# Another order of the quads, other banks and more raw tiles in the gate blocks of a mixer kernel; one gate job moved

## The chip, the cores and the metric

The kernel runs on one core of a Trainium2 chip. The metric is device time in microseconds (us). The kernel before took 2747.88 us, the median of three runs from 2747.08 to 2752.04.

## The reference, cut to what matters

One layer of a sequence mixer on x of 256 rows and 4096 columns, all in float32:

```
h = rms_norm(x)                                    # 256 x 4096
proj = h @ w_in                                    # 4096 x 22560, split by columns into
u, v, z_gm (2048 each), q k v of the delta rule (2048 each), z_dn, b, a, gate_gm, gate_dn (4096 each)
y_gm = (gelu(u) * spatial(layer_norm(gelu(v))) * silu(z_gm)) @ w_br_gmlp      # 2048 x 4096
y_dn = (rms_norm(gated_delta_rule(conv(q), conv(k), conv(v))) * silu(z_dn)) @ w_br_dn
x = x + (sigmoid(gate_gm) * y_gm + sigmoid(gate_dn) * y_dn) @ w_out           # 4096 x 4096
out = rms_norm(x)
```

## The kernel before, in words

All weights stream from HBM once. A product in float32 precision is made of three TensorE matmuls of a high and a low part: xh*wh, xh*wl and xl*wh. A raw weight tile holds 128 x 1024 numbers (0.5 MB); ScalarE casts it to the high part `wh` and VectorE subtracts to make the low part `wl` (`split`, L182 to L188; in the gate blocks `cut`, L254). The 256 rows of x are the stationary operand, in two halves m of 128, so a matmul covers 128 x 128 by 512 columns and adds into one PSUM bank. There are eight banks: six in the pool `pm` (name `acc`) and two in `ps` (name `side`, handed out by `bank()`). The small matmuls of the other stages use `side`.

`stream` (L279) works through a list of jobs, cut into pieces. An ordinary `Job` is 512 columns of a weight: a piece is one raw tile, 12 matmuls, and a job of 4096 rows has 16 pieces in two banks. A `Block` is a pair of gate jobs, 1024 columns, worked through in 16 quads of 256 rows (two raw tiles). A quad named in `SEVEN` is computed with seven products in place of eight: `quad_split` (L258) forms sums and differences of the raw quarters on VectorE (L263, L264, L268, L269) and four pieces a, b, d, c bring 3 + 6 + 6 + 6 matmuls with prepared sums of x (`gforms`). Any other quad has two pieces, n0 and n1, of 12 matmuls. A block thus has 8 x 21 + 8 x 24 = 360 matmuls in eight accumulators, P1 to P8 (`block_acc`, L203); n pieces use P8, P4, P2, P3. Before, the quads of seven are 0, 2, ..., 14, so a block begins with a quad of seven and ends with one of eight. `sums_out` (L984) adds the eight accumulators into four outputs as each of them gets its last matmul: P1, P6, P7, P5 (twice), P4, P2, P3, P8 (L990 to L998).

`make` (L318) splits pieces ahead of the matmuls: up to four pieces (not counting a) and five pieces of the list, in four tiles each of `wh` and `wl`. `get` (L294) issues the raw loads on SyncE's queue (SP), in order, up to a number of tiles ahead, into five tiles `raw` of pool `wp` and, for blocks alone, one more of pool `px`. A raw tile is given back when the last piece that reads it is split.

All other work is written as generators in two queues, `lanes`; after each 12 matmuls `step` (L122) advances the head of each queue by one yield. Lane 0 holds what follows each job (`done_...`), lane 1 the delta rule (`ba_gen`, `dn_gen`). The written order is not the issued order: a planner that simulates the program arranges the instructions of each engine, by its own estimate of when each is ready, and gives out the slots of a pool as they come free.

The order of jobs: two gate jobs (0, 2), six blocks (12 gates), four groups of v, k, q and z_dn of the delta rule, four jobs v, then u and z_gm four times in turn, gates 13 and 15, sixteen jobs `w_br_...` and eight jobs `w_out`. A v job's `done_v` is followed, after the last one, by `ln_gen` (L517), which normalizes `vg` when `open_b` (L478), at the end of the last `dn_gen`, has opened the pool `pb`; `done_u` calls `need_b` (L495), which steps the lanes until then. `done_z` multiplies 128 x 128 matrices with `vg` (L576). `done_gate` (L971) takes the sigmoid and stores the gate. Gate 13 opens the last pool, `pc` (`open_c`, L1024), and queues the loads of the eight tiles `yr` (L1034), their casts (L1037) and differences (L1039), which the jobs `w_br_...` use as `ys`.

Of the kernel before, what the change touches and what calls it, by code (L numbers as in the profile page):

```python
# [17 lines left out]
P = 128  # L18
# [11 lines left out]
SUB = 32  # L30
TAIL = 5
WARM = 9
SEVEN = tuple(range(0, 16, 2))


class Job:
# [25 lines left out]
def trunk(ctx, tc, t):  # L62
# [25 lines left out]
    upr = cst.tile([P, P], F32, name="upr")  # L88
    low = cst.tile([P, P], F32, name="low")
    lowr = cst.tile([P, P], F32R, name="lowr")  # L90
    ones = cst.tile([P, P], F32, name="ones")
    half = cst.tile([P, 8], F32, name="half")
    rstd = cst.tile([P, 2], F32, name="rstd")
    dng = cst.tile([P, P], F32, name="dng")
# [11 lines left out]
    pres = {(q, g): dr.tile([S + 3, NC], F32, name=f"pre{q}{g}") for q in "kqv" for g in range(4)}  # L106
    sgs = [dr.tile([P, 2, NC], F32, name=f"sgs{c}") for c in range(16)]

    V.memset(ones, 1.0)
    V.memset(half, -0.5)  # L110

    def after(tiles, src):
# [87 lines left out]

    def block_acc():  # L203
        acc = {n: pm.tile([P, 512], F32, name="acc") for n in ("P1", "P6", "P7", "P5", "P4", "P2")}
        acc["P3"], acc["P8"] = bank(), bank()
        return acc

    def plain(job, k, m):
        a, r = job.src(k)
# [69 lines left out]
    def stream():  # L279
# [8 lines left out]
        for p in pieces:  # L288
            order += [r for r in p.raws if r not in order[-2:]]
        raws, home, sp, acc, late = {}, {}, {}, None, []  # L290
        room = {"wp": 5, "x": 1}
        state = dict(got=0, made=0, pairs=0, mm=0)

        def get(upto):  # L294
            while state["got"] < min(upto, len(order)):
                n = state["got"]
                j, k = order[n]
                quad = isinstance(j, Block)
                where = "wp" if room["wp"] else "x" if room["x"] and quad else None
                if where is None:  # L300
                    return
                if n > 3:
                    first_x(n)
                room[where] -= 1
                home[j, k] = where
                if not quad:
                    raws[j, k] = fetch(j, k, n == 0)
                else:
                    raw = (wp if where == "wp" else px).tile([P, KPD, NC], F32, name="raw",
                                                             bufs=5 if where == "wp" else 1)  # L310
                    nc.sync.dma_start(out=raw, in_=j.w[k * P:(k + 1) * P, j.col:j.col + 2 * NC].rearrange(
                        "p (c n) -> p c n", c=2))
                    raws[j, k] = raw
                if n < 4:
                    first_x(n)
                state["got"] += 1

        def make():  # L318
            p = pieces[state["made"]]
            n = order.index(p.raws[-1])  # L320
            get(n + (4 if p.kind == "std" else 5))
            if state["made"] == 0:
                sp[0] = split0(raws[p.raws[0]])
            elif p.kind == "std":
                split_x(state["made"])
                sp[state["made"]] = split(raws[p.raws[0]], state["made"] >= len(pieces) - TAIL)
            else:
                sp[state["made"]] = quad_split(p, [raws.get(r) for r in p.raws])
            for r in p.retire:
                raws.pop(r)  # L330
                room[home.pop(r)] += 1
            state["made"] += 1
            state["pairs"] += p.kind != "a"
# [637 lines left out]
    def done_gate(i):  # L971
        def f(acc):
            z = (pc.tile([P, 2, NC], F32, name="sg", bufs=4) if pc else
                 pb.tile([P, 2, NC], F32, name="gu", bufs=2) if pb else px.tile([P, 2, NC], F32, name="sg", bufs=3))

            def gen():
                for m in range(2):
# [46 lines left out]
    def open_c():  # L1024
        nonlocal pc
        done_by()
        phv.close()
        phb.close()
        pc = phc.enter_context(tc.tile_pool(name="pc", bufs=1, reuse_waits="tile"))

        def gen():
            for i in range(8):
                yr = pc.tile([P, 4, S], F32, name="yr", bufs=1)
                nc.sync.dma_start(out=yr, in_=(ygs + yds)[i])  # L1034
                ys[i] = pc.tile([P, 2, 4, S], F32R, name=f"ys{i}")
                yield 2
                A.copy(ys[i][:, 0], yr)  # L1037
                yield
                V.tensor_tensor(out=ys[i][:, 1], in0=yr, in1=ys[i][:, 0].bitcast(F32), op=ALU.subtract)  # L1039
                yield  # L1040
        lanes[1].append(gen())

    sig, part = {}, {}

    def before_br(i):
        def f():
            sig[i] = pc.tile([P, 2, NC], F32, name="sg", bufs=4)
            nc.sync.dma_start(out=sig[i], in_=sgs[i])
        return f

    def done_br(i):
        d, second = i // 2, i % 2

        def f(acc):
            s = sig.pop(i)

            def gen():
                for m in range(2):
                    V.tensor_tensor(out=s[:, m], in0=acc[m], in1=s[:, m], op=ALU.mult)
                if not second:  # L1060
                    part[d] = s
                    yield
                    return
# [1 line left out]
                for m in range(2):  # L1065
                    V.tensor_tensor(out=s[:, m], in0=s[:, m], in1=q[:, m], op=ALU.add)
                yield
                tt = pc.tile([P, 2, 4, P], F32, name="yr", bufs=1)
                for m in range(2):
                    sm, ms = heads(s[:, m]), slice(m * P, (m + 1) * P)  # L1070
                    yield from turn(sm, sm, tt[:, m])
# [101 lines left out]
    for c in range(4):  # L1173
        jobs.append(Job(win, U0 + c * NC, KT, xsrc, done_u(c)))
        jobs.append(Job(win, ZG0 + c * NC, KT, xsrc, done_z(c)))
    for i in (13, 15):
        jobs.append(Job(win, GD0 + i // 2 * NC, KT, xsrc, done_gate(i), open_c if i == 13 else None))
    for i in range(16):
        d, second = i // 2, i % 2
        jobs.append(Job(t["w_br_dn"] if second else t["w_br_gmlp"], d * NC, KT // 2,  # L1180
                        (lambda k, s=second * 4: (ys[s + k // 4], k % 4)), done_br(i), before_br(i)))
    for c in range(8):
# [55 lines left out]
```

## Time and profile before

| | |
|---|---|
| runs | 2747.08, 2747.88, 2752.04 us |
| the profiled execution | 2753.06 us, its span 2751.3 us |
| busy share of the span | TensorE 98%, weight loads 80%, VectorE 67%, ScalarE 53%, GpSimd 1% |
| mean granted TensorE clock | 0.996 |
| HBM | 569.16 MB read, 24.19 MB written, 216 GB/s |

Every time below is from the profiled execution, counted from the start of its span. A row of a timeline gives start, duration, engine, line, operation, output and inputs, and in brackets how long the engine was idle before it and what released it. A matmul's start is recorded; its end is modelled, and matmuls overlap, so the distance of starts tells how fast they run.

### The profile page before, as it was taken

The page shows a single profiled execution, that of the slowest core. Times are in us where ns is not written, and L with a number is a line of the kernel's source. Part 1 is how long each engine was busy: PE and PEld are TensorE (multiplying, and loading weights), DVE is VectorE, ACT ScalarE, POOL GpSimd, SP SyncE. Part 2 cuts the span into 40 slices and gives each one's busy share as a digit, 9 for nine tenths or more (in the row PEclk, how much of TensorE's full clock was granted, in tenths as well). Part 3 has the DMA queues.
Part 4 walks back from the last instruction along what each step waited for, and adds up shares of the span by engine and source line. Part 5 has one row for each costly group of instructions (what it writes and reads, how often), then busy time and mean ns, then how long its engine had stood idle before and what let it go on. Part 6 is the DMA issues. An engine that isn't in the chain of part 4 may idle for free.

```text
span 2751.3 us, 33611 instructions
## 1 busy us (share of the span) xinstructions
PE 2697.4 (98%) x12241; PEld 2208.1 (80%) x12241; DVE 1843.7 (67%) x2476; ACT 1453.0 (53%) x2023; POOL 40.1 (1%) x40
## 2 busy tenths in 40 slices
PE   9999999999999999999999999999999999999998
PEld 7777777788878778778878887888888888888886
DVE  8788888886676867865885656645556666655544
ACT  7555555554564555554655545545544655644443
POOL 0000000000000000000010000000000000000000
PEclk9999999999999999999999999999999999999999
DMA  9666666568777777875875666676776666576665
GB/s 352 198 192 202 202 206 216 177 218 263 220 225 236 239 221 219 260 215 168 294 201 171 199 182 198 193 207 198 218 273 211 224 214 219 177 243 216 207 215 168
DMA packets 300719, 595.58 MB, mean 216 GB/s; under 512 B 33636, under 2 KB 47972, under 8 KB 300168
## 3 DMA queue, kind: packets, MB, share of 16 engines
q1 hardware_dynamic: 300264, 593.28, 68.7%
q8 instruction: 96, 1.57, 0.2%
q14 instruction: 71, 0.58, 0.1%
q10 hardware_dynamic: 288, 0.15, 0.0%
HBM read 569.16 MB, written 24.19 MB: 216 GB/s over the span
## 4 chain that ended last, share of the span: by engine, by line
PE 67%; DVE 12%; DMA 12%; issue 4%; ACT 3%; SPq 1%; POOL 0%; DVEq 0%; POOLq 0%; ACTq 0%
PE acc L198 20%; PE acc L197 20%; PE acc L199 20%; DMA raw<-w_in 6%; DVE wl L256 3%; DVE wl L187 2%; PE acc L235 1%; PE acc L236 1%; PE acc L234 1%; DMA tok<-preq 1%; ACT wh L186 1%; DMA preq<-tok 1%; DVE tok L712 1%; DVE tt L264 1%; PE side L235 1%
## 5 line engine op out<-in xcount | busy, mean ns | idle before, releaser
L187 DVE TENSOR_TENSOR wl<-raw,wh 128x1024 fp32r<-128x1024 f32 x762 | 925.8, 1221 | 655.3 <-ACT wh L186 652.0
L186 ACT CAST wh<-raw 128x1024 fp32r<-128x1024 f32 x762 | 794.9, 1052 | 893.5 <-PE acc L199 822.0
L198 PE MATMUL acc<-wl,xs 128*128 128x512 f32 x2540 | 993.7, 391 | 9.3 <-DVE wl L187 9.1
L199 PE MATMUL acc<-wh,xs 128*128 128x512 f32 x2540 | 990.4, 390 | 0.0
L197 PE MATMUL acc<-wh,xs 128*128 128x512 f32 x2540 | 984.5, 392 | 5.7 <-ACT wh L186 5.3
L198 PEld LDWEIGHTS acc<-wl,xs 128*128 128x128 f32 x2540 | 478.0, 188 | 115.4 <-DVE wl L187 17.8
L197 PEld LDWEIGHTS acc<-wh,xs 128*128 128x128 f32 x2540 | 477.2, 188 | 108.1 <-ACT wh L186 8.7
L199 PEld LDWEIGHTS acc<-wh,xs 128*128 128x128 f32 x2540 | 477.7, 188 | 98.9
L198 PE MATMUL acc<-wl,ys 128*128 128x512 f32 x512 | 199.2, 389 | 0.0
L199 PE MATMUL acc<-wh,ys 128*128 128x512 f32 x512 | 199.2, 389 | 0.0
L255 ACT CAST wh<-raw 128x1024 fp32r<-128x1024 f32 x144 | 149.4, 1050 | 92.3 <-PE side L236 77.3
L197 PE MATMUL acc<-wh,ys 128*128 128x512 f32 x512 | 195.8, 389 | 0.0
L256 DVE TENSOR_TENSOR wl<-raw,wh 128x1024 fp32r<-128x1024 f32 x144 | 172.3, 1220 | 10.1 <-ACT wh L255 9.8
L235 PE MATMUL acc<-wl,xs 128*128 128x512 f32 x288 | 114.2, 396 | 4.1 <-DVE wl L256 4.0
L256 DVE TENSOR_TENSOR wl<-tt,wh 128x1024 fp32r<-128x1024 f32 x96 | 116.3, 1219 | 1.9 <-ACT wh L255 1.8
L236 PE MATMUL acc<-wh,xs 128*128 128x512 f32 x288 | 112.8, 392 | 0.0
L197 PEld LDWEIGHTS acc<-wh,ys 128*128 128x128 f32 x512 | 96.1, 188 | 20.1
L198 PEld LDWEIGHTS acc<-wl,ys 128*128 128x128 f32 x512 | 96.1, 188 | 19.9
L199 PEld LDWEIGHTS acc<-wh,ys 128*128 128x128 f32 x512 | 96.1, 188 | 19.9
L255 ACT CAST wh<-tt 128x1024 fp32r<-128x1024 f32 x96 | 99.3, 1047 | 21.6 <-PE acc L236 12.1
L234 PE MATMUL acc<-wh,xs 128*128 128x512 f32 x288 | 97.4, 392 | 0.0
L255 ACT CAST s<-raw 128x512 fp32r<-128x512 f32 x48 | 29.8, 621 | 125.0 <-DMA raw<-w_in 125.0
(270 smaller groups left out, 2308.2 us busy)
## 6 DMA issues: line engine op xcount, KB each, us to landing
raw<-w_in SPq DMA_DIRECT2D x703, 512.0 KB
raw<-w_out SPq DMA_DIRECT2D x128, 512.0 KB
raw<-w_br_gmlp SPq DMA_DIRECT2D x64, 512.0 KB
raw<-w_br_dn SPq DMA_DIRECT2D x64, 512.0 KB
cw<-conv_w SPq DMA_DIRECT2D x48, 256.0 KB
sgs<-sg SPq DMA_DIRECT2D x16, 512.0 KB
sg<-sgs SPq DMA_DIRECT2D x16, 512.0 KB
tok<-prev SPq DMA_DIRECT2D x12, 512.0 KB
```

The source lines that it names most:

```text
L186: A.copy(h, raw)
L187: V.tensor_tensor(out=l, in0=raw, in1=h.bitcast(F32), op=ALU.subtract)
L197: T.matmul(acc[m], lhsT=xh, rhs=h[:, kk], start=f, stop=False)
L198: T.matmul(acc[m], lhsT=xh, rhs=l[:, kk], start=False, stop=False)
L199: T.matmul(acc[m], lhsT=xl, rhs=h[:, kk], start=False, stop=e)
L234: T.matmul(acc[name], lhsT=xh, rhs=h[:, i], start=f, stop=False)
L235: T.matmul(acc[name], lhsT=xh, rhs=l[:, i], start=False, stop=False)
L236: T.matmul(acc[name], lhsT=xl, rhs=h[:, i], start=False, stop=e)
L255: A.copy(h, src)
L256: V.tensor_tensor(out=l, in0=src, in1=h.bitcast(F32), op=ALU.subtract)
L264: V.tensor_tensor(out=t12[:, 1], in0=t12[:, 0], in1=r1[:, 0], op=ALU.subtract)
L712: V.tensor_tensor(out=h[:, m], in0=h[:, m], in1=cw, op=ALU.mult)
```

## The change

Six edits. `SEVEN` becomes 1, 3, 4, 6, 8, 9, 11, 13: still eight quads, but a block begins with quad 0 and ends with quads 14 and 15 of eight products, and 3, 4 and 8, 9 are neighbours. `block_acc` takes P3 and P8 from `side` in odd blocks and P6 and P7 in even ones, and asks for the banks in another order. Pool `px` has three raw tiles in place of one, and `get` looks two tiles further ahead in blocks. Gate 13 runs between the last v and the first u, with its output tile in pool `pv`, and gate 15 opens `pc`. The `yr` tiles become two, their generator has two yields per tile in place of four and begins with the tiles of the delta rule; the `w_br_dn` job of each pair runs first, and the second `w_br` job waits until all of that generator has been written. The unused tile `ones` and its memset go.

```diff
-SEVEN = tuple(range(0, 16, 2))
+XRAW = 3
+SEVEN = (1, 3, 4, 6, 8, 9, 11, 13)
-    ones = cst.tile([P, P], F32, name="ones")
-    V.memset(ones, 1.0)
+    nblk = [0]
     def block_acc():
-        acc = {n: pm.tile([P, 512], F32, name="acc") for n in ("P1", "P6", "P7", "P5", "P4", "P2")}
-        acc["P3"], acc["P8"] = bank(), bank()
-        return acc
+        nblk[0] += 1
+        apart = ("P6", "P7") if nblk[0] % 2 == 0 else ("P3", "P8")
+        return {n: bank() if n in apart else pm.tile([P, 512], F32, name="acc")
+                for n in ("P8", "P4", "P2", "P3", "P1", "P6", "P5", "P7")}
-        room = {"wp": 5, "x": 1}
+        room = {"wp": 5, "x": XRAW}
-                                                             bufs=5 if where == "wp" else 1)
+                                                             bufs=5 if where == "wp" else XRAW)
-            get(n + (4 if p.kind == "std" else 5))
+            get(n + (4 if p.kind == "std" else 4 + XRAW))
@@ done_gate
-                 pb.tile([P, 2, NC], F32, name="gu", bufs=2) if pb else px.tile([P, 2, NC], F32, name="sg", bufs=3))
+                 pv.tile([P, 2, NC], F32, name="sg") if pv else px.tile([P, 2, NC], F32, name="sg", bufs=3))
@@ open_c
-            for i in range(8):
-                yr = pc.tile([P, 4, S], F32, name="yr", bufs=1)
+            for i in (4, 5, 6, 7, 0, 1, 2, 3):
+                yr = pc.tile([P, 4, S], F32, name="yr", bufs=2)
                 nc.sync.dma_start(out=yr, in_=(ygs + yds)[i])
                 ys[i] = pc.tile([P, 2, 4, S], F32R, name=f"ys{i}")
-                yield 2
+                yield
                 A.copy(ys[i][:, 0], yr)
-                yield
                 V.tensor_tensor(out=ys[i][:, 1], in0=yr, in1=ys[i][:, 0].bitcast(F32), op=ALU.subtract)
                 yield
+                if i == 3:
+                    ys["all"] = True
@@ before_br
+            while i == 0 and "all" not in ys:
+                step()
@@ done_br
-                if not second:
+                if second:
-                tt = pc.tile([P, 2, 4, P], F32, name="yr", bufs=1)
+                tt = pc.tile([P, 2, 4, P], F32, name="yr", bufs=2)
@@ jobs
-    for i in (13, 15):
-        jobs.append(Job(win, GD0 + i // 2 * NC, KT, xsrc, done_gate(i), open_c if i == 13 else None))
+    jobs.insert(len(jobs) - 8, Job(win, GD0 + 6 * NC, KT, xsrc, done_gate(13)))
+    jobs.append(Job(win, GD0 + 7 * NC, KT, xsrc, done_gate(15), open_c))
     for i in range(16):
         d, second = i // 2, i % 2
+        second = 1 - second
+        i = 2 * d + second
```

## Rows read from the trace of the kernel before

**Rows 1.** The page's busy times: us, share of the span, instructions.
```profile
PE 2697.4 (98%) x12241; PEld 2208.1 (80%) x12241; DVE 1843.7 (67%) x2476; ACT 1453.0 (53%) x2023; POOL 40.1 (1%) x40
```

**Rows 2.** Windows: six blocks, first, last, w_out jobs. Stretch, length, busy (instructions), clock, DMA.
```profile
94.60:625.40 530.80, 509.30 (x2165) 403.72 (x2164) 450.84 (x522) 286.54 (x315) 0.00 (x0) 1.00 0.63 201
94.60:186.10 91.50, 86.12 (x361) 66.50 (x360) 71.89 (x84) 45.66 (x51) 0.00 (x0) 1.00 0.59 185
539.50:625.40 85.90, 84.00 (x365) 67.88 (x364) 76.37 (x87) 48.65 (x53) 0.00 (x0) 1.00 0.66 209
2478.00:2652.00 174.00, 174.00 (x769) 144.07 (x768) 87.56 (x81) 72.91 (x80) 0.00 (x0) 1.00 0.66 212
```

**Rows 3.** Waits of SyncE's queue, whole span: us in total, times, longest.
```profile
SPq L311 <- DVE wl L256: 258.0, 137, 7.0
SPq L311 <- DVE tt L268: 155.4, 45, 8.5
```

**Rows 4.** Waits of the engines in the first block, 94.6 to 186.1 us.
```profile
ACT s L255 <- DMA raw<-w_in: 37.7, 8, 6.9
PE acc L235 <- DVE wl L256: 4.6, 9, 0.9
```

**Rows 5.** Waits of the engines in the other five blocks, 186.1 to 625 us.
```profile
ACT s L255 <- DMA raw<-w_in: 83.3, 32, 6.4
ACT wh L255 <- PE side L236: 77.1, 58, 2.4
PE side L234 <- DVE sg L998: 8.9, 5, 1.9
```

**Rows 6.** Timeline of VectorE in the first block.
```profile
112.89 1.22 DVE L256 TENSOR_TENSOR wl<-raw,wh 128x1024 fp32r<-128x1024 f32 x1
114.03 0.69 DVE L256 TENSOR_TENSOR s<-raw,s 128x512 fp32r<-128x512 f32 x1
114.63 1.22 DVE L256 TENSOR_TENSOR wl<-tt,wh 128x1024 fp32r<-128x1024 f32 x1
```

**Rows 7.** Timeline at the first border between two blocks.
```profile
189.40 0.40 PE L236 MATMUL acc<-wh,gf 128*128 128x512 f32 x1
...
190.89 0.69 DVE L998 TENSOR_TENSOR sg<-side,sg 128x512 f32<-128x512 f32 x1
...
191.73 0.77 PE L234 MATMUL side<-wh,gf 128*128 128x512 f32 x1 [1.93 <-DVE sg L998]
...
192.29 0.63 PE L235 MATMUL side<-wl,gf 128*128 128x512 f32 x1
...
192.72 0.63 PE L236 MATMUL side<-wh,gf 128*128 128x512 f32 x1
```

**Rows 8.** Windows: around that border; the jobs u1 and z1.
```profile
180.00:200.00 20.00, 17.32 (x68) 13.48 (x67) 18.90 (x24) 12.54 (x15) 0.00 (x0) 0.91 0.73 238
...
1677.90:1730.60 52.70, 48.10 (x210) 39.66 (x209) 43.55 (x74) 34.11 (x67) 3.28 (x3) 0.94 0.66 218
1730.60:1776.60 46.00, 45.92 (x210) 37.99 (x209) 21.41 (x25) 26.25 (x41) 0.00 (x0) 1.00 0.69 204
```

**Rows 9.** Timeline of TensorE in job u1.
```profile
1715.86 2.05 PE L576 MATMUL side<-vg,wst 128*128 128x128 f32 x8 [4.60 <-DVE vg L543]
```

**Rows 10.** Line L857 of the delta rule: shortest, median, longest ns, first and last start.
```profile
L857 PE MATMUL side<-tmp,nt x128: 191/191/212, 982.2 to 1623.9; 32*32 32x32 f32 x128
```

**Rows 11.** Timeline where the last delta rule ends and the normalization of v begins.
```profile
1694.84 0.51 SPq L965 DMA_DIRECT2D yds<-vtok  x1
...
1697.69 1.26 ACT L556 ACTIVATE gu<-acc,rstd 128x512 f32<-128x512 f32 x2
...
1699.48 1.67 DVE L528 TENSOR_SCALAR vg<-vg,mu 128x512 f32<-128x512 f32 x4
```

**Rows 12.** Windows: the jobs of gates 13 and 15.
```profile
1954.30:1997.90 43.60, 43.60 (x195) 36.12 (x195) 26.73 (x38) 26.11 (x44) 0.00 (x0) 1.00 0.75 243
1997.90:2043.10 45.20, 44.10 (x194) 35.99 (x193) 25.34 (x22) 23.40 (x25) 0.00 (x0) 1.00 0.75 252
```

**Rows 13.** Groups by line, 1954 to 2043 us: busy, mean ns, idle before.
```profile
L186 ACT CAST wh<-raw 128x1024 fp32r<-128x1024 f32 x32 | 32.4, 1050 | 15.6 <-PE acc L199 15.5
...
L1037 ACT CAST ys<-yr 128x1024 fp32r<-128x1024 f32 x8 | 8.4, 1052 | 22.4 <-DMA yr<-yds 12.1 <-DMA yr<-ygs 10.2
```

## The prediction

> **What bounds the kernel now.** I read the busy line of the page first, then windows of TensorE by stage, and only then the waits and timelines of the stages in which those windows lose something. By the busy line TensorE is the bound: 98% [rows 1]. That share flatters, because a matmul is recorded as some 390 ns long and its successor starts earlier, so a short hole is hidden. The windows tell more if one divides their length by the count of matmuls. In the w_out jobs, where nothing is late, it is 174 us / 768 = 0.2266 us per matmul; in the six gate blocks 530.8 us hold 2165, which at 0.2266 would take 490.6 us [rows 2]. So the blocks lose 40.2 us. The change removes no matmul (still eight quads of 21 and eight of 24 per block), so it can win only what is lost: these 40.2, and what the moved gate touches.
>
> Why the blocks lose it: nothing computes at its limit. VectorE, spaced as in its timeline, needs 1.14 us for a 1024-wide difference and 0.60 for a 512-wide one [rows 6]. A quad of seven has five of the short and three of the long, 6.4 us; a quad of eight two of the long, 2.3; with eight sums at the end that is 8 x 8.7 + 4.8 = 74.4 us a block, against 360 x 0.2266 = 81.6 us of matmuls. What is short is raw tiles. SyncE stands 258.0 + 155.4 = 413 us before a load, for VectorE to give a tile back [rows 3], in a stretch of 531; at the other end ScalarE waits for raw data at 40 of the 48 quads of seven, 37.7 us in the first block and 83.3 in the others [rows 4, 5]. The first block shows it pure: no accumulators stand before it, and it still takes 91.5 us, 9.9 over its matmuls [rows 2], TensorE held by late low parts [rows 4]. In the later blocks a second wait comes on top, at each of the five borders: the new block's first use of a `side` bank waits for the last sums of the old one, 8.9 us in five [rows 5]. At the first border the pause of 1.93 us also drops TensorE to its lower level (1.2 GHz): the next matmuls start 0.43 us apart, and the granted clock of that slice is 0.91 [rows 7, 8].
>
> **The change part by part.**
>
> *Three raw tiles in `px`, and a look-ahead to match.* Six tiles turn over 192 loads in 530.8 us [rows 2], so one tile is held 6 x 530.8 / 192 = 16.6 us from issue to release. Eight tiles held as long would pass one load per 2.07 us; matmuls want one per 490 / 192 = 2.55. The limit moves from 13% over the matmul time to 19% under it. No byte is added: the stretch moves 201 GB/s at a DMA share of 0.63 [rows 2].
>
> Against taking that room for free speaks the Trainium skill. Its page "DMA: Bandwidth & Descriptors" (section "Latency and other measured facts") puts the access time of HBM at 0.2 us on average and 2 us at high load. By it a tile could be held 1.8 us longer, an estimate, and eight tiles would pass a load per 18.4 / 8 = 2.3 us, still under 2.55; no row here shows the landing at a higher load.
>
> *Other banks.* A block now starts with n pieces, in P8, P4, P2, P3. P1, P6, P7, P5 got their last matmul in quad 13, and their sums can run beside quads 14 and 15. After an odd block those four sit in `pm`, which is where the even block wants P8, P4, P2, P3; after an even block P1, P5 are in `pm` and P6, P7 in `side`, where the odd block wants P4, P2 and P3, P8. Each first use finds a bank long free, and the five waits go, with the slow matmuls behind the first. What is late next is quad 1, 24 matmuls or 5.4 us later, by when four sums (2.4 us) have freed the other four banks.
>
> Against it stands a rule of the Trainium skill ("TensorE: Matmul & The Clock Gate", section "A second HAM failure mode: psum-queue depth-cycling"): a kernel that cycles through banks each iteration can idle TensorE often enough to lose its clock again and again. By it the blocks would lose more. Here the matmuls already go from bank to bank every three, and the granted clock over the blocks is 1.00 [rows 2]; the one dip stands at a wait, not at a change of bank. I give it no share.
>
> *The order of the quads.* VectorE's heavy end (sums) now meets three quads of eight in a row, 16.3 us of matmuls against 6.9 us of splitting and 4.8 of sums. The price is at 3, 4 and 8, 9: two quads of seven need 12.9 us of VectorE in 42 x 0.2266 = 9.5 us. The missing 3.4 must come out of the lead, up to four split pieces. That there is such a lead I read from ScalarE, which waits 77.1 us, 58 times, for TensorE to free a `wh` tile [rows 5]: it is usually as far ahead as it may be. So I put this at nothing; without cover it is 12 places x 3.4 = 41 us.
>
> Together these edits are worth between 0 and 40.2 us. The last block, with its border and its end in it, takes 85.9 us for 365 matmuls [rows 2], 3.2 over; so most of a loss can go even with six tiles. I take 1.5 us left per block, 9 in all: **-31 us**.
>
> *Gate 13 between v and u.* In job u1 TensorE stands 4.60 us before L576, for the normalized v [rows 9], at a clock of 0.94; u1 takes 52.7 us and z1, of equal count, 46.0 [rows 8]: 6.7 us. The normalization follows the last delta rule, which is written step by step until `need_b` at the end of u0 writes out the rest at once. From its solver's products (last at 1623.9, the end of u0) to its last store (1694.8) it takes 71 us [rows 10, 11], for some 39 yields in the code. With one more job ahead of `need_b`, 16 of these go at the pace of the jobs (43.5 us) and 23 at 71 / 39 = 1.8, 42 us: it ends near 1624 + 43.5 + 42 = 1710 in place of 1695, and v is ready near 1731 in place of 1716. But z0, which needs it, ends near 1678 + 45 = 1723 in place of 1678, and its products are written after its own SiLU and further back in the lane. The wait shrinks from 4.60 us to little or none; bounds 0 and 6.7, I take **-5**, nearer to the window's whole price since a short wait keeps the clock. The sigmoid of gate 13 adds ScalarE work beside half-idle jobs: 0.
>
> *One gate and two `yr` tiles behind `open_c`.* Gates 13 and 15 took 43.6 + 45.2 = 88.8 us there [rows 12], 1.8 over two times 43.5, with ScalarE waiting 22.4 us in eight parts for the `yr` loads [rows 13]. All eight now fall into one gate: 16 casts of 1.05 us, eight copies of 1.05 and, if no wait shrinks, 22.4 make 47.6 us for a job of 43.5, 4.1 us late. If two tiles hide the loads, 1.8 is won. The first `w_br_dn` job needs only `ys` 4 to 7 in its 21.8 us, so the loads themselves are early. Between -1.8 and +4.1 I take **0**, near the loss that two gates showed.
>
> *The memset of `ones`* is one short VectorE operation in the first microseconds; the swapped branches have equal counts: 0.
>
> The sum is -36 us. Against the profiled execution (2753.1, of it span 2751.3) it gives 2717.1; that execution lies 5.2 over the median of the runs, so against the median it is 2747.9 - 36 = **2711.9, say 2712 us**.
>
> **The rivals.**
>
> *A. Only the borders go.* Loads take as much longer as there are more of them in flight, or three `px` tiles are freed in an order that `get`, strictly in order, cannot use; then quads inside a block stay raw-limited. For it: the loads are bunched, two tiles freed together. Against it: DMA share 0.63. It wins the five waits (8.9), some 1 us of hidden overlap with them and 2 us of slow matmuls, 12 in all, and the 5 of u1: 2747.9 - 17 = 2731 us.
>
> *B. The neighbours 3, 4 and 8, 9 cost what the rest wins.* Lead at quad 3 is gone after quad 1, and 12 places lose 3.4 us: 41 against the 40.2 won. Against it the 77.1 us of ScalarE's waits. Time: 2747.9 - 5 + 1 = 2744 us, no change.
>
> *C. Slower: u1 stands for banks.* Gate 13, u0 and z0 fill all six `pm` banks, and u1 needs gate 13's two. Its sigmoid is written behind `ln_gen` in lane 0. If the planner leaves it there, u1 (due near 1723) stands until the normalization is over: 16 us at least (v ready 1731, its last parts and the sigmoid to 1739), and up to 69 us if the 39 + 19 steps go at the jobs' pace of 2.7 us. It decides from 31 us on; at its upper end the time is 2747.9 - 31 + 69 = 2786 us. Against it: the planner issued u0's GELU at 1697.7, before the normalization's first parts at 1699.5, though it is written behind them [rows 11].
>
> **How the numbers follow.** Forecast 0.68, A 0.19, B 0.09, C 0.04. The forecast's own range is 2702 to 2724: all that can be won is 40.2 + 6.7 + 1.8 = 48.7 (2699), and 12 of the 36 may be missing, since the planner rearranges every stage. A reaches from 2724 to 2738. For 8 in 10 the range is 2701 to 2737: nearly all of the forecast and most of A. About 0.2%, 5.5 us, is what a measurement can tell from no change: faster is forecast, A and a little of B, 0.89; same is most of B, 0.06; slower is C and a part of B, 0.05.
>
> **What would show it.** Right: six blocks in 495 to 505 us of windows; no wait of TensorE for L998; SyncE's wait for raw tiles still long, but ScalarE's wait for raw data below 40 us in place of 121; u1 as long as z1. A would show 515 us with ScalarE's waits unchanged; B, TensorE waiting for low parts at quads 4 and 9; C, a hole at the start of u1. Wrong altogether would be a longer stretch from the blocks' end to v, or a gate 15 above 50 us.

## The result and the profile after

| | before | after |
|---|---|---|
| median of the runs, us | 2748.99 (4 runs, 2747.08 to 2752.04) | 2722.74 (4 runs, 2719.90 to 2727.94) |
| profiled execution, us | 2753.06, span 2751.3 | 2727.94, span 2725.8 |

The ratio is 0.9906 with a 95% interval of 0.9886 to 0.9925: 26 us faster, inside the range and 11 us short of the forecast. The total came out nearly as said; the experiments show that half of the reasons did not.

The page of the kernel after, busy times (us, share of the span, instructions), the row that answers to [rows 1]:

```profile
PE 2688.8 (99%) x12241; PEld 2211.5 (81%) x12241; DVE 1843.5 (68%) x2475; ACT 1460.1 (54%) x2025; POOL 39.9 (1%) x40
```

The work is the same. Windows of the kernel after (columns as in [rows 2]): the six gate blocks, the stretch from the first job K0 to the end of v3, the jobs u1 and z1, and gate 15.

```profile
96.00:593.00 497.00, 497.00 (x2162) 405.47 (x2161) 448.92 (x520) 290.54 (x315) 0.00 (x0) 1.00 0.69 213
636.50:1555.60 919.10, 901.65 (x4289) 739.68 (x4288) 641.49 (x1015) 488.34 (x723) 28.52 (x18) 0.99 0.72 221
1697.70:1752.10 54.40, 48.57 (x214) 39.99 (x213) 39.63 (x74) 38.31 (x84) 1.65 (x2) 0.94 0.67 217
1752.10:1796.30 44.20, 44.20 (x200) 36.70 (x199) 21.78 (x18) 22.57 (x23) 0.00 (x0) 1.00 0.72 209
1974.60:2018.20 43.60, 43.60 (x195) 36.10 (x194) 32.69 (x43) 31.58 (x49) 0.00 (x0) 1.00 0.85 296
```

And the second of these stretches in the kernel before, which the rows ahead of the prediction do not have:

```profile
668.20:1579.40 911.20, 897.83 (x4289) 737.73 (x4288) 640.72 (x1015) 488.13 (x723) 28.52 (x18) 1.00 0.73 223
```

The blocks take 497.0 us in place of 530.8 [rows 2], 33.8 less, and TensorE is busy from end to end. At 0.2266 us a matmul the 2161 would take 489.7, 7.3 less; by the same count the kernel before lost 41 (40.2 by the count of the prediction). These 7.3 us are no wait: each of the six blocks takes 82.8 us, 0.2300 us for each of its 360 matmuls, with no hole. So the yardstick from the `w_out` jobs was a little short for the blocks, whose matmuls start 0.2300 us apart at a granted clock of 1.00; why is open. What could be won was 34 us, and all of it was. Nothing else moved much for the better: u1 is 1.7 us longer than in [rows 8], z1 1.8 shorter, gates 13 and 15 together (43.50 + 43.60) 1.7 shorter than in [rows 12]. The stretch from K0 to v3, which the change does not touch, is 7.9 longer in this pair of profiles. In the profiles of all 14 kernels here the instructions of TensorE, VectorE and ScalarE come in one and the same order in this stretch, and it takes anywhere between 910.4 and 919.1 us; the two of this pair stand near the ends. So the difference is put down to the executions, and sizes below are taken from medians and block windows, not from this pair of spans.

Waits of the engines inside the blocks of the kernel after (engine, tile and line, what it waited for: us, times, longest), against [rows 4, 5]:

```profile
ACT wh L258 <- PE acc L239: 77.4, 93, 2.2
ACT s L258 <- DMA raw<-w_in: 64.8, 43, 3.8
ACT wh L258 <- PE side L239: 44.6, 44, 2.2
PEld side L238 <- DVE wl L259: 0.3, 1, 0.3
```

No matmul waits any more (0.3 us before one weight load is left); ScalarE waits for TensorE, which is how a stage bound by TensorE looks. SyncE's queue still waits long before a load of a raw tile (same columns, whole span; [rows 3] had 258.0 and 155.4):

```profile
SPq L314 <- DVE wl L259: 254.0, 137, 6.6
SPq L314 <- DVE tt L271: 135.6, 46, 6.3
```

That wait fell by 24 us of 413 while the loss fell by 34 of 41. It was read as the sign of what is short; it stays when nothing is short, because the code issues each load as soon as a tile is free, so the queue stands before most loads at any pace. ScalarE's wait for raw data, said to fall below 40 us from 121, is still 64.8 in blocks that lose nothing, so that sign was badly chosen too.

In u1 the hole did not go. TensorE's timeline (start, duration, and in brackets the idle time before and who ended it), to set against [rows 9]:

```profile
1728.84 2.04 PE L579 MATMUL side<-vg,wst 128*128 128x128 f32 x8 [5.83 <-DVE vg L546]
```

### The profile page after: what moved, and what is told of

Read it like the earlier page. It is cut to its first block, busy times and chain, and to the rows that moved or that the text cites. A ratio compares the mean times of both kernels' runs of the same rounds, so it can differ in the third digit from the quotient of the medians.

```text
span 2725.8 us, 33592 instructions
## 1 busy us (share of the span) xinstructions
PE 2688.8 (99%) x12241; PEld 2211.5 (81%) x12241; DVE 1843.5 (68%) x2475; ACT 1460.1 (54%) x2025; POOL 39.9 (1%) x40
## 4 chain that ended last, share of the span: by engine, by line
PE 61%; issue 25%; DMA 6%; DVE 4%; ACT 2%; SPq 0%; POOL 0%; POOLq 0%; DVEq 0%; ACTq 0%
PE acc L197 20%; PE acc L196 20%; PE acc L198 20%; DVE wl L186 2%; DMA tok<-preq 1%; ACT wh L185 1%; DMA raw<-w_in 1%; DMA cw<-conv_w 1%; DMA preq<-tok 1%; ACT kT L154 1%; DVE tok L715 1%; DMA tok<-prek 0%; DVE tok L716 0%; PE side L579 0%; DMA tok<-prev 0%
## 5 line engine op out<-in xcount | busy, mean ns | idle before, releaser
L197 PE MATMUL acc<-wl,xs 128*128 128x512 f32 x2540 | 995.6, 392 | 14.0 <-DVE wl L186 13.5
L198 PE MATMUL acc<-wh,xs 128*128 128x512 f32 x2540 | 991.6, 391 | 0.0
L196 PE MATMUL acc<-wh,xs 128*128 128x512 f32 x2540 | 984.9, 392 | 4.9 <-ACT wh L185 4.1
L197 PEld LDWEIGHTS acc<-wl,xs 128*128 128x128 f32 x2540 | 478.5, 188 | 122.2 <-DVE wl L186 24.7
L198 PEld LDWEIGHTS acc<-wh,xs 128*128 128x128 f32 x2540 | 478.5, 188 | 98.6
L259 DVE TENSOR_TENSOR wl<-raw,wh 128x1024 fp32r<-128x1024 f32 x144 | 174.0, 1222 | 10.2 <-ACT wh L258 9.9
L238 PE MATMUL acc<-wl,xs 128*128 128x512 f32 x384 | 150.3, 391 | 0.0
L239 PE MATMUL acc<-wh,xs 128*128 128x512 f32 x384 | 149.9, 390 | 0.0
L237 PE MATMUL acc<-wh,xs 128*128 128x512 f32 x384 | 125.0, 391 | 0.0
L238 PEld LDWEIGHTS acc<-wl,xs 128*128 128x128 f32 x384 | 72.1, 188 | 16.1
```

The lines of the kernel that those rows point to most:

```text
L196: T.matmul(acc[m], lhsT=xh, rhs=h[:, kk], start=f, stop=False)
L197: T.matmul(acc[m], lhsT=xh, rhs=l[:, kk], start=False, stop=False)
L198: T.matmul(acc[m], lhsT=xl, rhs=h[:, kk], start=False, stop=e)
L237: T.matmul(acc[name], lhsT=xh, rhs=h[:, i], start=f, stop=False)
L238: T.matmul(acc[name], lhsT=xh, rhs=l[:, i], start=False, stop=False)
L239: T.matmul(acc[name], lhsT=xl, rhs=h[:, i], start=False, stop=e)
```

## The experiments

Each was timed beside the kernel before; the gains below are median against the median of before that was timed with it (2750.47, 2751.04, 2750.49 or 2750.85 us). "Blocks" is the window from the first matmul of the blocks to the last. Edits are shown against the kernel named.

**Only six raw tiles** (after):

```
-XRAW = 3
+XRAW = 1
```

> The changed kernel with one raw tile in px and the old look-ahead; order of quads and banks stay new. Theory T, raw tiles carry the loss inside the blocks: six tiles pass a load per 2.77 us where matmuls want 2.55, so the six blocks, 497 us in the changed kernel, return to 520 to 545 us, with ScalarE's and VectorE's waits for raw data back above 150 us, and the kernel takes 2745 to 2770 us. Rival R, the borders (order and banks) carried the gain: blocks at most 505 us, the kernel 2723 to 2731 us.

Measured: 2730.25 us (2726.44 to 2733.05), ratio 0.9929 (0.9917 to 0.9942), a gain of 20.2.

```profile
94.40:601.50 507.10, 501.80 (x2162) 405.81 (x2161) 448.94 (x521) 290.36 (x317) 0.00 (x0) 1.00 0.66 211
```

With the old number of tiles most of the gain stays; the blocks come out 2 us above the bound of R. The theory of the prediction, that six tiles held 16.6 us each are the limit, gave 2745 to 2770 and falls. The tiles turn over in less time as soon as the order is another; how long they are held was a result, not a constant.

**Old order of the quads** (after):

```
-SEVEN = (1, 3, 4, 6, 8, 9, 11, 13)
+SEVEN = tuple(range(0, 16, 2))
```

> The changed kernel with the quads of seven at 0, 2, ..., 14 again; eight raw tiles and the alternating banks stay. Theory T: inside the blocks nothing is lost (eight tiles), but an even block wants P6 and P7 from side in its first quad, where P3 and P8 of the odd block still wait for their sums; three borders of 2 to 4 us and two easier ones: blocks 503 to 515 us, the kernel 2729 to 2741 us. Rival R, the order matters only for VectorE's load and the banks alone cure the borders: blocks below 501, the kernel within 4 us of the changed one, 2719 to 2727 us.

Measured: 2736.50 us (2734.63 to 2742.84), ratio 0.9956 (0.9944 to 0.9969), a gain of 14.0. The window of its blocks and then TensorE's waits in them:

```profile
96.30:609.40 513.10, 503.65 (x2162) 404.02 (x2161) 449.93 (x520) 285.78 (x315) 0.00 (x0) 1.00 0.67 205
```

```profile
PEld acc L238 <- DVE wl L259: 5.9, 11, 1.5
...
PE acc L237 <- DVE sg L1001: 3.8, 2, 2.3
PE side L237 <- DVE sg L1001: 2.9, 2, 1.4
```

Some 2.0 to 2.7 us are lost at each border again, at the new block's first two quads, though the banks are the new ones. The first block, which has no border before it, is 2.4 us longer too, against the 82.8 of the changed kernel:

```profile
96.30:181.50 85.20, 84.00 (x361) 67.31 (x360) 73.15 (x84) 47.42 (x53) 0.00 (x0) 1.00 0.66 198
```

**Old banks** (after):

```
-        apart = ("P6", "P7") if nblk[0] % 2 == 0 else ("P3", "P8")
-        return {n: bank() if n in apart else pm.tile(...) ...}
+        acc = {n: pm.tile([P, 512], F32, name="acc") for n in ("P1", "P6", "P7", "P5", "P4", "P2")}
+        acc["P3"], acc["P8"] = bank(), bank()
+        return acc
```

> The changed kernel with the old bank assignment: P3 and P8 in side in every block, six others in pm. Theory T: quad 0 now begins with P8 and P3, and both banks are freed by the last two sums of the block before, some 3 us after its last matmul; five borders of 2.5 to 5 us (the longer ones with slow matmuls behind them): blocks 510 to 522 us, the kernel 2735 to 2748 us, with TensorE waiting for the sum of P8 5 times. Rival R, with enough raw tiles and three quads of eight at the border the sums are early: blocks at most 502, the kernel 2719 to 2728 us.

Measured: 2722.63 us (2721.88 to 2724.18), ratio 0.9903 (0.9889 to 0.9916): a gain of 27.8, that of the whole change. Theory T falls: the blocks take 497.2 us, and TensorE waits for no bank in them.

```profile
95.70:592.90 497.20, 497.20 (x2161) 405.86 (x2160) 450.78 (x521) 291.11 (x315) 0.00 (x0) 1.00 0.70 214
```

**Eight raw tiles alone** (before):

```
+XRAW = 3
-    ones = cst.tile([P, P], F32, name="ones")
-    V.memset(ones, 1.0)
-        room = {"wp": 5, "x": 1}          # and the tile's bufs, and the look-ahead
+        room = {"wp": 5, "x": XRAW}
```

> The kernel before with three raw tiles in px and the longer look-ahead alone (and without the unused tile, for room). Theory T: the loss inside the blocks goes (9.9 us of the first block to 1 or 2), the five borders stay with 2 to 4 us each: blocks 505 to 515 us in place of 530.8, the kernel 2728 to 2738 us (-11 to -21). Rival R, the raw-limited pace is set elsewhere (VectorE's order, landing times that grow with the loads in flight): blocks above 522 us, the kernel 2740 to 2752 us.

Measured: 2735.24 us (2733.18 to 2739.46), ratio 0.9947 (0.9934 to 0.9961), a gain of 15.2.

```profile
96.90:608.70 511.80, 504.54 (x2163) 407.45 (x2162) 449.90 (x521) 288.28 (x316) 0.00 (x0) 0.99 0.68 206
```

The loss inside the blocks goes, as T said: the first block takes 84.0 us in place of 91.5 [rows 2]. The border stays. Here is TensorE there, and then VectorE in the 4 us before (start, duration, line, tiles):

```profile
187.22 0.47 PE L233 MATMUL side<-wh,gf 128*128 128x512 f32 x1 [1.99 <-DVE sg L997]
```

```profile
183.45 0.69 DVE L267 TENSOR_TENSOR tt<-raw,tt 128x512 f32<-128x512 f32 x1
184.06 0.68 DVE L268 TENSOR_TENSOR tt<-raw,tt 128x512 f32<-128x512 f32 x1
184.66 1.22 DVE L255 TENSOR_TENSOR wl<-raw,wh 128x1024 fp32r<-128x1024 f32 x1
185.79 0.68 DVE L262 TENSOR_TENSOR tt<-raw 128x512 f32<-128x512 f32 x1
186.40 0.68 DVE L997 TENSOR_TENSOR sg<-side,sg 128x512 f32<-128x512 f32 x1
```

Each starts before the recorded end of the one ahead of it: no hole. The sum L997, which frees the bank, comes behind splitting for quads that follow. The same place with the new order and the old banks, VectorE in the old-banks kernel:

```profile
180.04 1.22 DVE L257 TENSOR_TENSOR wl<-tt,wh 128x1024 fp32r<-128x1024 f32 x1
181.17 0.68 DVE L999 TENSOR_TENSOR sg<-side,sg 128x512 f32<-128x512 f32 x1
181.77 0.68 DVE L996 TENSOR_TENSOR sg<-acc,sg 128x512 f32<-128x512 f32 x1
182.37 0.68 DVE L997 TENSOR_TENSOR sg<-acc,sg 128x512 f32<-128x512 f32 x1
182.97 0.68 DVE L998 TENSOR_TENSOR sg<-side,sg 128x512 f32<-128x512 f32 x1
```

There all four sums are through by 183.7 us, and TensorE has matmuls on other banks until 184.08, when it first uses a `side` bank for the new block:

```profile
184.08 0.39 PE L235 MATMUL side<-wh,xs 128*128 128x512 f32 x1
```

The `side` banks are free, by 0.4 us, without having been exchanged.

**Banks alone** (before, with the new `block_acc`):

> The kernel before with the alternating banks alone. Theory T, the border's price is VectorE's backlog (the last sums stand behind the splitting of the next quads of seven), not the bank: blocks 526 to 535 us as before, with the waits moved from the sum of P8 to late low parts, the kernel 2746 to 2754 us. Rival R, the forecast's step: the five waits go, blocks 516 to 521 us, the kernel 2736 to 2741 us.

Measured: 2753.47 us (2750.01 to 2760.27, 12 runs), ratio 1.0010 (1.0001 to 1.0018). Window of the blocks, and TensorE's longest wait in them:

```profile
94.10:622.60 528.50, 509.28 (x2162) 403.16 (x2162) 448.75 (x520) 284.27 (x314) 0.00 (x0) 1.00 0.63 201
```

```profile
PE acc L239 <- DVE wl L260: 11.4, 17, 1.2
```

The wait for the sums is gone, as the prediction said, and TensorE stands for low parts instead, which the same VectorE makes. Nothing is won.

**Order alone** (before, with the new `SEVEN`; six raw tiles, old banks):

> The kernel before with the new order of the quads of seven alone: six raw tiles, old banks. Theory T, the order does nearly all that order and banks did with six raw tiles (2730): blocks 504 to 510 us, lost only at the neighbours 3, 4 and 8, 9, no wait at the borders, the kernel 2727 to 2734 us. Rival R, with six tiles the old banks still hold a block's first matmuls: blocks 514 to 522 us, the kernel 2737 to 2744 us.

Measured: 2727.77 us (2725.85 to 2737.48, 6 runs), ratio 0.9924 (0.9910 to 0.9937), a gain of 23.3. The blocks, and SyncE's waits for a tile, against [rows 3]:

```profile
93.90:596.10 502.20, 499.13 (x2161) 404.84 (x2160) 449.26 (x521) 291.58 (x317) 0.00 (x0) 1.00 0.67 213
```

```profile
SPq L311 <- DVE wl L256: 288.3, 138, 7.2
SPq L311 <- DVE tt L268: 75.5, 44, 4.7
```

One line of the change, which the prediction put at nothing, brings most of it. The waits for the tiles that L268 gives back halve, from 155.4 to 75.5, while the others rise by 30. What is left, some 5 us over the blocks of the change, stands in three of the six blocks (the first, the second and the last, 85.5, 84.0 and 84.2 us), mostly one and two quads behind a pair of neighbouring quads of seven, by the count of matmuls, 0.3 to 2.2 us at each. Two things stay open. The first block, which has no sums before it, also gains, from 91.5 to 85.5 us, and the border cannot be the reason. And six tiles with the new banks as well (the first experiment) do no better than this kernel with the old ones: gains of 20.2 and 23.3, with intervals that overlap.

**Three quads of eight behind, seven ahead** (after):

```
-SEVEN = (1, 3, 4, 6, 8, 9, 11, 13)
+SEVEN = (0, 2, 3, 5, 7, 8, 10, 12)
```

> The changed kernel with the quads of seven at 0, 2, 3, 5, 7, 8, 10, 12: a block begins with a quad of seven but ends with three of eight; neighbours are 2, 3 and 7, 8. Theory T, what counts at a border is VectorE's backlog, and three quads of eight in a row carry it wherever the border lies among them: blocks 496 to 500 us, no wait of TensorE for sums, the kernel within 4 us of the changed one (2719 to 2727 us). Rival R, a block must begin with a quad of eight (its first accumulators are those freed last, or its first split is the long one behind the sums): 2 to 3 us at each border, blocks 506 to 515 us, the kernel 2730 to 2740 us.

Measured: 2725.78 us (2725.17 to 2726.76), ratio 0.9914 (0.9900 to 0.9927), blocks 498.8 us, 1.8 of the difference in the first block. No border loses anything: the five later blocks take 414.1 us, as in the changed kernel (414.2). So it matters that three quads of eight stand together around the sums, not that the block begins with one.

**A lighter border** (eight raw tiles alone, and the first quad of every block leaves out the two differences of `t34`, so the gates' values differ):

```
+            light = p.k == 0
+            t34 = t12 if light else px.tile([P, 2, NC], F32, name="tt", bufs=3)
+            if not light:
                 V.tensor_tensor(out=t34[:, 0], in0=r0[:, 1], in1=t12[:, 1], op=ALU.subtract)
                 V.tensor_tensor(out=t34[:, 1], in0=r1[:, 1], in1=t12[:, 1], op=ALU.subtract)
```

> The kernel before with three raw tiles in px (the kernel of the run with raw tiles alone, 2735 us), in which the first quad of each block, a quad of seven, leaves out its two last differences (two of 512 columns, 1.2 us of VectorE, just ahead of the old block's last sums) and uses the first pair of sums in their place; so the gates' values are wrong. Nothing changes in banks, loads, casts or matmuls. Theory T, the border is VectorE's backlog: the holes at the five borders, 2.8 to 5.2 us a block before, shrink by 1.2 us or more each, blocks 499 to 506 us in place of 512, the kernel 2727 to 2732 us. Rival R, the border waits for something that VectorE's load does not set (the last matmuls of the old block, the banks): within 2 us of 2735.

Measured: 2730.53 us (2729.28 to 2733.25), ratio 0.9927 (0.9914 to 0.9941). The blocks, and TensorE's waits in them:

```profile
96.10:602.10 506.00, 502.21 (x2163) 404.07 (x2162) 444.55 (x510) 287.36 (x315) 0.00 (x0) 1.00 0.67 208
```

```profile
PE side L234 <- DVE wl L255: 3.7, 10, 0.6
...
PEld acc L233 <- DVE sg L997: 1.2, 5, 0.3
```

Against the kernel with raw tiles alone, which waited longer for this sum:

```profile
PE side L233 <- DVE sg L997: 4.4, 4, 2.0
```

Five borders times two differences of 0.60 us [rows 6] are 6.0 us of VectorE; the blocks became 5.8 shorter (511.8 to 506.0), the median some 5. So VectorE's load at the border does set a loss (the edit also gives raw and `tt` tiles back a little earlier, which this run does not tell apart). The near equality is no rule of one for one, though. The later blocks became shorter by very unequal amounts, 0.1 to 2.3 us, where T said 1.2 or more at each border; and some 3.2 of the 5.8 us are two stretches of eight matmuls at the lower level (1.2 GHz), 0.43 us apart in place of 0.23, behind the first and third border of the kernel with raw tiles alone, which this kernel has none of:

```profile
180.90:267.70 86.80, 84.81 (x362) 68.69 (x360) 76.02 (x91) 47.76 (x54) 0.00 (x0) 0.98 0.70 207
...
352.30:439.20 86.90, 84.95 (x361) 68.71 (x360) 76.62 (x91) 48.31 (x54) 0.00 (x0) 0.98 0.70 208
```

**Gate 13 back beside gate 15** (after):

```
-    jobs.insert(len(jobs) - 8, Job(win, GD0 + 6 * NC, KT, xsrc, done_gate(13)))
-    jobs.append(Job(win, GD0 + 7 * NC, KT, xsrc, done_gate(15), open_c))
+    jobs.append(Job(win, GD0 + 6 * NC, KT, xsrc, done_gate(13), open_c))
+    jobs.append(Job(win, GD0 + 7 * NC, KT, xsrc, done_gate(15)))
```

> The changed kernel with gate 13 back beside gate 15, behind the last z; it opens pc again. Theory T, the planner puts the products with the normalized v (the matmuls behind done_z) where by its own estimate v is ready, and the chip is 5 to 6 us later wherever that is: TensorE waits 4 to 7 us in u1 in this order too, and the kernel is within 3 us of the changed one (2719 to 2726 us). Rival R, the forecast's step: the gate between v and u is worth some 5 us in another way, and this kernel takes 2726 to 2731 us.

Measured: 2721.32 us (2718.85 to 2722.35), ratio 0.9891 (0.9876 to 0.9905). Job u1 takes 52.8 us with a hole of 4.48, as before (52.7 and 4.60). The move of the gate is worth nothing.

**Products written later** (after; the normalized v's products are tied in TensorE's order behind the matmul last written, and come ten steps later in c = 0):

```
-                yield
+                yield 10 if c == 0 else 1
+                    with tc.issue_after(last_mm[0].ins):
                         for i in range(4): ... T.matmul(b[...], lhsT=wst[:, g], rhs=vg[m][...])
```

> The changed kernel with the first products with the normalized v written ten steps later and all of them tied, in TensorE's queue alone, behind the last matmul written before them (58 matmuls or 13 us later than in the changed kernel). Theory T, the wait is only a too early place in TensorE's queue: it goes (under 1 us in place of 5.8), u1 takes 47 to 49 us in place of 54.4, and the kernel 2714 to 2718 us. Rival R, what hangs on the products (the z tiles, side banks, the lane behind them) is late as well: a like wait shows elsewhere in u1 to z1, and the kernel stays at 2720 to 2727 us.

Measured: 2722.61 us (2722.14 to 2724.39), ratio 0.9899 (0.9886 to 0.9912). TensorE in its u1, and VectorE over the hole:

```profile
1723.08 0.80 PE L198 MATMUL acc<-wl,xs 128*128 128x512 f32 x1 [6.75 <-DVE wl L187]
```

```profile
1711.56 1.23 DVE L187 TENSOR_TENSOR wl<-raw,wh 128x1024 fp32r<-128x1024 f32 x1 [1.56 <-ACT wh L186]
...
1715.90 5.39 DVE L545 SCALAR_TENSOR_TENSOR vg<-vg,r,lng 128x512 f32<-128x512 f32 x8 [0.90 <-POOL r L116]
1721.20 0.68 DVE L547 TENSOR_TENSOR vg<-vg,lnb 128x512 f32<-128x512 f32 x1
1721.81 1.22 DVE L187 TENSOR_TENSOR wl<-raw,wh 128x1024 fp32r<-128x1024 f32 x1
```

The products are out of the way and the hole is as long, now before an ordinary matmul of u1 that has no low part. Between the split at 1711.56 and the one at 1721.81 VectorE makes none: eight products of the normalization, 5.39 us, stand in its queue in one piece, and before them it waits for ScalarE's squares (1.85 us) and for GpSimd (0.90). That the products came too early in TensorE's order was my first theory; it falls.

**The normalization spread** (after; each product of the normalization tied in VectorE's order behind the last split):

```
-        yield 2
+        yield 13
+                with tc.issue_after(last_sub[0].ins):
                     V.scalar_tensor_tensor(out=v, in0=v, scalar=r2[:, m:m + 1], ...)
                     V.tensor_tensor(out=v, in0=v, in1=lnb[...], op=ALU.add)
```

> The changed kernel with the second half of the normalization of v (eight products and eight sums on VectorE) tied in VectorE's queue, one pair behind each split of a raw tile, where it stood as eight products in a row. Theory T, the hole of u1 is made by that row: for some 9 us VectorE makes no low part, so a later place of TensorE's products did not help, and v was ready late because eight products stood ahead of the first sum. Spread out, the hole shrinks to 0 to 2 us, u1 takes 47 to 50 us in place of 54.4, and the kernel 2714 to 2719 us. Rival R, VectorE needs the same time in all and only loses later (z1 longer by as much), or TensorE still stands at the products: 2720 to 2726 us.

Measured: 2717.64 us (2716.02 to 2720.00), ratio 0.9884 (0.9870 to 0.9897), the fastest of the study together with the next kernel. Windows of its u1 and z1, and VectorE in u1:

```profile
1696.20:1745.80 49.60, 47.74 (x225) 39.52 (x224) 39.99 (x72) 38.36 (x82) 1.65 (x2) 1.00 0.71 230
1745.80:1789.30 43.50, 43.50 (x193) 36.04 (x192) 21.52 (x21) 22.61 (x26) 0.00 (x0) 1.00 0.76 221
```

```profile
1721.16 1.42 DVE L546 SCALAR_TENSOR_TENSOR vg<-vg,r,lng 128x512 f32<-128x512 f32 x2 [0.90 <-POOL r L116]
1722.49 0.69 DVE L548 TENSOR_TENSOR vg<-vg,lnb 128x512 f32<-128x512 f32 x1
1723.10 1.22 DVE L187 TENSOR_TENSOR wl<-raw,wh 128x1024 fp32r<-128x1024 f32 x1
```

u1 and z1 take 93.1 us in place of 98.6, and the granted clock of u1 is 1.00 where it was 0.94. The interval of the ratio overlaps that of the change itself, and the two were not timed side by side; the 5.5 us of the windows and the 5 us between the medians agree.

**Both** (the last two edits together):

> The kernel with the spread normalization and, besides, the products with the normalized v tied behind a later matmul in TensorE's queue (84 matmuls, 19 us later than in the changed kernel). Theory T: both holes are closed, the one for v and the one for low parts; u1 and z1 lose nothing beyond their side matmuls, u1 46 to 48 us, the kernel 2713 to 2717 us. Rival R: as with the products held alone, a hole for low parts of 5 to 7 us stays, the kernel 2720 to 2726 us.

Measured: 2718.12 us (2715.95 to 2720.74), ratio 0.9885 (0.9872 to 0.9899); u1 and z1 take 93.8 us, with a hole of 2.78 in u1, now for a low part; the time lies between T and R. Later products add nothing. What is left of the hole, 1.85 and 2.78 us in these two kernels, is open: VectorE stands idle for ScalarE's squares before it (1.86 us in the spread kernel), and spreading the subtraction as well was not tried.

## Why the prediction was right in its sum and wrong in its parts

*The loss and its size: right.* The blocks were said to lose 40.2 us and to get back 31; the windows say 33.8 of 41. Dividing the length of a window by its matmuls found the stage that the busy line hid. That the parts added up to a total inside the range is partly luck: the part that was put at nothing brought most of it, and the parts that were given the gain overlap with it or are worth nothing.

*"Eight raw tiles move the limit": true of the old order alone.* The step took six times 530.8 over 192 as the time for which a tile is held, and carried it over to eight. With the old order eight tiles do clear the inside of the blocks, but the time is no property of the tile: order alone gets the blocks to 502.2 with six. Tiles are worth 15 us alone; once the order is new, 5.0 by block windows and 4.5 by gains with the old banks (kernels that differ in the gate and the `yr` tiles too), 10 and 6 with the new. (The working also has a slip: 16.6 us over six tiles is 2.77 us a load, 8% over the 2.55 of the matmuls and not 13%.)

*"The banks free the border": failed.* The wait named was real, and the new banks take it away in the kernel that has only them, but the time is the same to 0.1%. [Rows 5] showed who ended the wait, VectorE's L998. I asked which bank was needed, and not why that sum was so late; VectorE's rows at the border answer that.

*"The order of the quads: nothing": this is the step that failed worst.* Its working had the answer. With the old order a border has one quad of eight and one of seven, 45 x 0.2266 = 10.2 us of matmuls, for 2.3 + 6.4 + 4.8 = 13.5 of VectorE: 3.3 short, 16.5 over five borders. Old order against new, all else equal, measures 513.1 - 497.0 = 16.1 us by the block windows, 2.4 of it in the first block, which has no border, and 13.7 in the other five, 2.1 to 3.4 each; by the gains it is some 12. So the sum gives the cause and the size of the loss, but it was made after the result, over two quads; over four (14, 15, 0, 1) the same numbers leave 22.2 - 20.4 = 1.8 us a border. I worked out the new order's surplus and the price of its neighbours, but not the shortage of the old one. With six tiles the order is worth more, 530.8 - 502.2 = 28.6 us by windows, 23 by gains. That a backlog on VectorE frees tiles late as well, so that loads are late too, would fit the halved wait of SyncE; no run shows it by itself. The parts overlap: 23 and 15 us alone, 28 together (the old-banks kernel, which has the moved gate and the two `yr` tiles as well).

*The price at the neighbours, 41 us without cover: the cover held.* With eight tiles nothing is lost there; with six, small losses at and behind them. (Two quads of seven need 12.8 us and not 12.9, so the price without cover is 3.3 us a place and 40 in all.)

*"Gate 13 between v and u: -5": measured 0.* Two steps failed. The first is the pace of the delta rule's end. It was to end 15 us later than before while z0 moved by a whole job. Where its solver's products and its last store stand after (form and times of the first; the second is a pair of DMA issues), against [rows 10, 11]:

```profile
L860 PE MATMUL side<-tmp,nt x128: 191/191/212, 952.1 to 1632.8; 32*32 32x32 f32 x128
```

```profile
1702.69 4.22 SPq L968 DMA_DIRECT2D yds<-vtok  x2
```

Counted from the end of v3 (1579.4 before, 1555.6 after) the solver moved from 44.5 to 77.2 us, and the last store from 115 to some 151 (the pair ends at 1706.9). So the end came 33 to 36 us later and not 15: few of the steps were taken sooner. That still left 7 us or more to gain. The second step is that the products stay where they are in u1: they start 31.1 us behind its start (1728.84 - 1697.7) where it was 38.0 (1715.86 - 1677.9), so the planner moved them forward by 7 us. And the wait had another cause than distance: VectorE's queue, as the spread normalization showed. The hole is 5.83 us in place of 4.60.

*One gate and two `yr` tiles: 0 forecast, -1.7 measured*, near the lower bound of -1.8. ScalarE's wait for `yr` fell from 22.4 us [rows 13] to 3.7, and gate 15 takes 43.6.

*The rivals.* A is refuted at its root: borders and raw tiles are not two losses that go apart. B and C did not happen; u1 waited for VectorE, not for a bank. (The 69 us of C do not come out of the numbers beside them: 58 steps of 2.7 us from 1624 end near 1781, 58 us behind 1723.) Of the two rules of the Trainium skill weighed in the prediction neither showed a cost here. For "DMA: Bandwidth & Descriptors" (section "Latency and other measured facts"): no trace here shows when a load landed; at 213 GB/s in place of 201 ScalarE's wait for raw data fell from 121 us to 64.8. For "TensorE: Matmul & The Clock Gate" (section "A second HAM failure mode: psum-queue depth-cycling"): the granted clock of the blocks is 1.00 with alternating banks as without (497.0 and 497.2 us).

*The signs.* Blocks in 495 to 505 us and no wait for the last sum came true. ScalarE's wait for raw data below 40 us and u1 as long as z1 did not. The longer stretch from the blocks' end to v, named as a sign of being wrong altogether, stands in this pair of profiles, and is put down to the executions.

*Left over.* The blocks' windows shrank by 33.8 us, the medians by 26. In this pair of profiles the stretch from K0 to v3 takes 7.9 back; between the medians the rest is not settled. Each window is that of one execution: banks alone, whose median is 2 us above before, has blocks of 528.5 where before has 530.8.

## What to carry to other kernels

When a wait names the engine that ended it, look at what stood in that engine's queue ahead of the instruction, before changing the buffer that was waited for: a bank freed late by a backlog is worth nothing until the backlog goes. Add up each engine's work over the few units around a border, not over a whole loop; here 74 of 82 us on average hid 13.5 against 10.2. And read a matmul's pace from the stage in question where it loses nothing: 0.2266 us from another stage was 1.5% under the pace of the blocks. A wait for free tiles at the load queue, and the time a tile is held, are results of the pace of the consumer and not its limit.

## What the runs showed of the hardware that was not expected

Pauses of one length had different ends. In the kernel before TensorE paused 1.93 us at the first border [rows 7] and 1.93 us again at the fourth, at the same line and for the same sum. Behind the first the next matmuls started 0.43 us apart, at the lower level (1.2 GHz); behind the fourth they did not:

```profile
455.37 0.47 PE L234 MATMUL side<-wh,gf 128*128 128x512 f32 x1 [1.93 <-DVE sg L998]
455.68 0.39 PE L235 MATMUL side<-wl,gf 128*128 128x512 f32 x1
```

A pause of 1.99 us in the kernel with raw tiles alone was followed by the lower level seven matmuls on (a clock of 0.91 in that slice, as in [rows 8]). A longer one, in the kernel with the old order, was not: the granted clock of its blocks is 1.00.

```profile
443.03 0.50 PE L237 MATMUL acc<-wh,gf 128*128 128x512 f32 x1 [2.29 <-DVE sg L1001]
```

In u1 of the changed kernel TensorE ran the eight products behind its hole of 5.83 us in 2.04 us and the next matmuls 0.43 apart; in the spread kernel, behind a hole of 1.85, it ran them in 1.13 and went on at 0.23, at a clock of 1.00. So in these traces a pause of some 2 us may or may not cost the clock, and its length alone does not tell.
